# A decoder trunk on one core: chunk 1's attention scores on two PSUM tiles instead of six

## The chip, the cores and the metric

The kernel runs on 1 core of one Trainium2 chip. The metric is the device time of one execution in microseconds (us); less is better. The engines that matter here are TensorE (PE, matmuls), VectorE (DVE), ScalarE (ACT) and GpSimd (POOL); SyncE (SP) issues most DMAs. Matmuls write into PSUM, which the kernel divides into eight tiles of 128 x 512 fp32.

## What is computed

A trunk of two layers on 256 tokens of width 1024. The first layer is a gated MLP over chunks, the second sparse attention with 16 heads in 4 groups. Both are followed by a squared-ReLU MLP of width 4096. Only the attention matters here. With 256 tokens the selected blocks and the window cover all earlier tokens, so that both branches are causal attention over their own keys; a third, small branch goes over compressed keys. Cut from the reference:

```python
def masked_softmax(s, mask):
    s = jnp.where(mask, s.astype(jnp.float32), -jnp.inf)
    m = jnp.max(s, axis=-1, keepdims=True)
    ...
    e = jnp.exp(s - m)
    den = jnp.sum(e, axis=-1, keepdims=True)
    return e / jnp.where(den > 0, den, 1.0)

def nsa_mixer(h, w_in, w_out, k_cmp, v_cmp, k_sel, v_sel, k_win, v_win):
    proj = h @ w_in
    q = proj[..., :HD].reshape(B, T, N_KV_HEADS, HEADS_PER_GROUP, HEAD_DIM) * (HEAD_DIM ** -0.5)
    ...
    s_sel = jnp.einsum('bqghd,bgqmd->bghqm', qb, ks)
    p_sel = masked_softmax(s_sel, kpos <= tq[None, None, None, :, None])
    o_sel = jnp.einsum('bghqm,bgqmd->bqghd', p_sel.astype(vs.dtype), vs)
    ...
    o = gb[..., 0:1] * ocb + gb[..., 1:2] * o_sel + gb[..., 2:3] * o_win
    ...
    return o @ w_out
```

## The kernel before

The 256 tokens are two chunks of 128 (ck = 0 and 1), each on the 128 partitions. Two generators, one for each chunk, run through the same stages, and `drive` (L973) takes turns between them: chunk 0 leads, chunk 1 follows some steps behind and uses the same weights. A scheduler then puts the instructions of each engine in order by priorities and by when it expects data and tiles to be there. So which PSUM tile an instruction waits for sets its place, too. Projections are made of three matmuls a product (`mm3`, L376 to L379: high part of the weight, low part of the weight, low part of the activations).

The eight PSUM tiles are three pools: `psY` with four (output sums, `oT` and `y`), `psA` with two (projections, `pa`; gates; compressed scores, `cs`) and `psT` with two (transposes). A tile of a pool is given out again when all that read its last owner are done.

The attention of a chunk (`nsa`, L921) has two halves p2, with two groups g each. A half goes through:

- `queries` (L780): a projection of 24 matmuls (`pa_bin` in psA), two copies of it (`qs`, high part on ACT at L786, low part on DVE at L787), transposes (`ptq`, L792) and their copies (`qT`).
- `scores` (L822), for each group: chunk 1 makes one score tile for each of four heads (h0 = 0 to 3), chunk 0 one for two heads (h0 = 0 and 2). A tile takes two matmuls against the keys of both branches (L838) and one for the causal mask (L840) per head. DVE takes the negative maxima (`mx`, L841), then ACT the exponentials with their sums (`p` and `den`, L845), one for each head and branch.
- `weighted` (L851): DVE scales p (L866), PE transposes it (`ptp`, L874), ACT copies that (`pT`, L876), and PE sums it with the values into `oT` (L879). The two groups of a half lie side by side as two column tiles of 64, so that their matmuls can run together.
- `attend_cmp` (L884): scores over compressed keys (`cs`, L891, in psA), their softmax on DVE, a transpose (`ptcm`), and a last addition to `oT` (L918).

Afterwards `oT` is split into two parts (`hh_o` on ACT, `hl_o` on DVE) and projected (`nsa_out`, L953, `y_mix`), and the feed-forward stage of the second layer follows.

The table `SY` says which score tiles (ck, g, h0) come from psY; all others come from psA (L833):

```python
sc = (psY.tile([P, per, 2, nk], F32, tag="y", name=f"sc_{ck}_{g}_{h0}") if (ck, g, h0) in SY else
      psA.tile([P, per, 2, nk], F32, tag="a", name=f"sc_{ck}_{g}_{h0}"))
```

The third field of an entry is the head; it is no count of tiles. Before, four tiles of chunk 0 and six of chunk 1 come from psY.

Of the kernel before, what the change touches and what calls it, by code (L numbers as in the profile page):

```python
# [41 lines left out]
PRIA = 100  # L42
PRIS = 150
RAW = 8
SY = [(0, 0, 2), (0, 1, 2), (0, 2, 0), (0, 3, 2), (1, 0, 2), (1, 0, 3), (1, 1, 2), (1, 1, 3), (1, 2, 1), (1, 3, 2)]
PRI = 30
FB = (13, 0.9)
RATES = (1.5, 0.69, 0.9, 0.13)
# [3 lines left out]
def trunk(ctx: ExitStack, tc: tile.TileContext, x, vec, rowv, first_w, ada_w, ada_b, norm_g, a_w_in, a_w_s, a_w_out,  # L52
# [364 lines left out]
    @contextmanager  # L417
    def prio(n):
        if n:
            with tc.high_priority(offset=n):  # L420
                yield
        else:
            yield
# [398 lines left out]
    def scores(ck, g, pool):  # L822
# [8 lines left out]
        for h0 in range(0, 4, per):  # L831
            with prio(PRIS):
                sc = (psY.tile([P, per, 2, nk], F32, tag="y", name=f"sc_{ck}_{g}_{h0}") if (ck, g, h0) in SY else  # L833
                      psA.tile([P, per, 2, nk], F32, tag="a", name=f"sc_{ck}_{g}_{h0}"))
# [283 lines left out]
```

## Time and profile before

| | us |
|---|---|
| median of three runs | 707.84 |
| lowest and highest | 706.71 and 709.61 |
| the profiled execution | 708.93 |
| its span, first to last instruction | 707.2 |

| engine | busy us | share |
|---|---|---|
| PE | 664.2 | 94% |
| DVE | 472.6 | 67% |
| ACT | 354.5 | 50% |
| POOL | 35.6 | 5% |

All times below are counted from the start of the span. The attention runs from about 386 us, when the first scores start, to about 495 us. Chunk 1's scores start at 417.6 us and end at 478 us. A row of the timeline gives the start, the duration, the engine, the line, the instruction with what it writes and reads, and in brackets how long the engine was idle before it and what released it; the profile leaves numbers out of the tiles' names. Matmuls are pipelined: the next one starts before the one ahead of it has ended, so that the distance of starts is what a matmul costs. "Granted clock" is TensorE's clock as a share of 2.4 GHz.

### The profile page before, as it was taken

How to read it: one execution, taken by the hardware profiler on the slowest of the kernel's cores; microseconds unless marked ns; L12 is line 12 of the kernel's file. 1: busy time of each engine (PE TensorE's matmuls, PEld its weight loads, DVE VectorE, ACT ScalarE, POOL GpSimd, SP SyncE). 2: the span in 40 equal slices, each digit the busy share in tenths (PEclk: the TensorE clock that was granted, in tenths of full speed). 3: DMA queues.
4: the chain of work that ended last, by engine and by line, in shares of the span. 5: the costliest groups of instructions: out<-in, count | busy, mean ns of one | idle time of the engine just before them, and what ended most of it. 6: DMA issues, size and time to landing. Idle time of an engine off the chain costs nothing.

```text
span 707.2 us, 9154 instructions
## 1 busy us (share of the span) xinstructions
PE 664.2 (94%) x3296; PEld 501.0 (71%) x3296; DVE 472.6 (67%) x712; ACT 354.5 (50%) x599; POOL 35.6 (5%) x70
## 2 busy tenths in 40 slices
PE   3999988999999999997899989979999999999996
PEld 1556856778888888876658556656778888888884
DVE  3557975997597786868975176754797545455524
ACT  4434435655534543463545386755556555455521
POOL 3002000100000000002000000000120000000000
PEclk9999999999999999998899999999999999999999
DMA  8978978779588988955675882200576656665101
GB/s 336 409 279 341 338 282 310 240 254 371 184 322 303 381 282 319 334 193 179 198 263 186 347 307 90 100 21 1 170 263 225 221 193 209 213 209 201 61 0 61
DMA packets 45535, 162.61 MB, mean 230 GB/s; under 512 B 5417, under 2 KB 5801, under 8 KB 45490
## 3 DMA queue, kind: packets, MB, share of 16 engines
q1 hardware_dynamic: 44928, 161.82, 63.0%
q8 instruction: 26, 0.43, 0.2%
q10 hardware_dynamic: 466, 0.20, 0.1%
q14 instruction: 19, 0.16, 0.1%
q0 software_dynamic: 96, 0.01, 0.0%
HBM read 160.96 MB, written 1.05 MB: 229 GB/s over the span
## 4 chain that ended last, share of the span: by engine, by line
PE 83%; ACT 6%; DMA 4%; DVE 3%; issue 2%; POOL 1%; SPq 0%; ACTq 0%; POOLq 0%; DVEq 0%
PE pa_fi L377 8%; PE pa_fi L379 8%; PE pa_fi L378 8%; PE y_ff L379 8%; PE y_ff L377 8%; PE y_ff L378 8%; PE pa_ain L377 2%; PE pa_ain L378 2%; PE pts_ff L490 2%; PE pa_ain L379 2%; DMA aw_sc<-in_ada_w_dram 2%; PE oT L879 2%; PE sc L838 2%; PE pa_kv L377 1%; PE pa_kv L378 1%
## 5 line engine op out<-in xcount | busy, mean ns | idle before, releaser
L353 DVE TENSOR_TENSOR wl_fo<-w_fo,wh_fo 128x1024 fp32r<-128x1024 f32 x64 | 77.9, 1223 | 54.2 <-ACT wh_fo L352 52.1
L378 PE MATMUL y_ff<-wl_fo,rh_ff 128*128 128x512 f32 x256 | 102.9, 402 | 0.0
L377 PE MATMUL pa_fi<-wh_fi,hh_ff 128*128 128x512 f32 x256 | 100.3, 392 | 1.9 <-ACT hh_ff L382 1.9
L377 PE MATMUL y_ff<-wh_fo,rh_ff 128*128 128x512 f32 x256 | 101.8, 398 | 0.0
L379 PE MATMUL y_ff<-wh_fo,rl_ff 128*128 128x512 f32 x256 | 101.3, 396 | 0.0
L352 ACT ACTIVATE wh_fo<-w_fo 128x1024 fp32r<-128x1024 f32 x64 | 67.3, 1057 | 67.6 <-PE pa_fi L379 50.9
L378 PE MATMUL pa_fi<-wl_fi,hh_ff 128*128 128x512 f32 x256 | 99.9, 390 | 0.0
L379 PE MATMUL pa_fi<-wh_fi,hl_ff 128*128 128x512 f32 x256 | 99.7, 391 | 0.0
L353 DVE TENSOR_TENSOR wl_fi<-w_fi,wh_fi 128x1024 fp32r<-128x1024 f32 x64 | 77.6, 1222 | 31.8 <-ACT wh_fi L352 31.3
L352 ACT ACTIVATE wh_fi<-w_fi 128x1024 fp32r<-128x1024 f32 x64 | 67.1, 1057 | 56.5 <-PE y_ff L379 49.5
L377 PEld LDWEIGHTS pa_fi<-wh_fi,hh_ff 128*128 128x128 f32 x256 | 48.1, 188 | 12.6 <-ACT hh_ff L382 2.8
L377 PEld LDWEIGHTS y_ff<-wh_fo,rh_ff 128*128 128x128 f32 x256 | 48.2, 188 | 10.8
L379 PEld LDWEIGHTS y_ff<-wh_fo,rl_ff 128*128 128x128 f32 x256 | 48.3, 189 | 10.2
L378 PEld LDWEIGHTS y_ff<-wl_fo,rh_ff 128*128 128x128 f32 x256 | 48.4, 189 | 10.0
L379 PEld LDWEIGHTS pa_fi<-wh_fi,hl_ff 128*128 128x128 f32 x256 | 48.1, 188 | 10.1
L378 PEld LDWEIGHTS pa_fi<-wl_fi,hh_ff 128*128 128x128 f32 x256 | 48.1, 188 | 9.9
L504 ACT ACTIVATE r_ff<-pa_fi 128x512 f32<-128x512 f32 x32 | 19.0, 594 | 35.7 <-PE pa_fi L379 35.7
L196 DVE SCALAR_TENSOR_TENSOR acc_g<-aw_g,cact,acc_g 128x1024 f32<-128x1024 f32 x24 | 30.7, 1281 | 5.0 <-DMA aw_g<-in_ada_w_dram 4.0
L845 ACT ACTIVATE p<-sc,mx 128x128 f32<-128x128 f32 (+1 forms) x64 | 26.0, 429 | 8.1 <-DVE mx L841 7.6
L377 PE MATMUL pa_ain<-wh_ain,hh_mix 128*128 128x512 f32 x64 | 26.4, 418 | 2.7 <-ACT hh_mix L382 2.7
L383 DVE TENSOR_TENSOR rl_ff<-pts_ff,rh_ff 128x512 fp32r<-128x512 f32 x32 | 21.9, 686 | 7.7 <-ACT rh_ff L382 7.5
L378 PE MATMUL pa_ain<-wl_ain,hh_mix 128*128 128x512 f32 x64 | 26.3, 414 | 0.0
(291 smaller groups left out, 1157.2 us busy)
## 6 DMA issues: line engine op xcount, KB each, us to landing
w_fi<-in_ff_w_in_dram SPq DMA_DIRECT2D x64, 512.0 KB, 4.7
w_fo<-in_ff_w_out_dram SPq DMA_DIRECT2D x64, 512.0 KB, 4.3
aw_g<-in_ada_w_dram SPq DMA_DIRECT2D x32, 512.0 KB, 4.5
aw_sh<-in_ada_w_dram SPq DMA_DIRECT2D x24, 512.0 KB, 5.3
aw_sc<-in_ada_w_dram SPq DMA_DIRECT2D x24, 512.0 KB, 6.0
aw_first<-in_first_w_dram SPq DMA_DIRECT2D x16, 512.0 KB, 7.7
w_ain<-in_a_w_in_dram SPq DMA_DIRECT2D x16, 512.0 KB, 7.2
w_kv<-in_kv_w_dram SPq DMA_DIRECT2D x12, 512.0 KB, 4.5
```

The costliest lines, as they stand in the source:

```text
L196: nc.vector.scalar_tensor_tensor(acc, raw, cs, acc, ALU.mult, ALU.add)
L352: i1 = nc.scalar.activation(hi[:, :n], raw[:, :n], AF.Copy)
L353: i2 = nc.vector.tensor_tensor(lo[:, :n], raw[:, :n], hi[:, :n].bitcast(F32), ALU.subtract)
L377: nc.tensor.matmul(ps, hh, wh, start=start, stop=False)
L378: nc.tensor.matmul(ps, hh, wl, start=False, stop=False)
L379: nc.tensor.matmul(ps, hl, wh, start=False, stop=stop)
L383: nc.vector.tensor_tensor(lo, src, hi.bitcast(F32), ALU.subtract))
L490: nc.tensor.transpose(pt[:, j * P:(j + 1) * P], src[:, j * P:(j + 1) * P], ident)
L504: nc.scalar.activation(r, pa, AF.Relu)
L838: nc.tensor.matmul(sc[:, i, :, :], qT[:, h0 + i, :], kT[:, g, hl, :, 0:nk], start=(hl == 0), stop=False)
L845: nc.scalar.activation(pr[h0 + i][:, br, :], sc[:, i, br, :], AF.Exp, bias=mx[:, 2 * i + br:2 * i + br + 1], accum_out=den[:, n:n + 1])
L879: m = nc.tensor.matmul(oT[64 * gg:64 * gg + 64, :], V[:, kc, br, g * 64:g * 64 + 64], pTs[gg][0], start=(br == 0 and kc == 0), stop=False)
```

## The change

Six entries of the table go, those of chunk 1. Its sixteen score tiles then all come from psA, which they share with the query projections of both chunks and the compressed scores. Chunk 0's entries stay.

```diff
-SY = [(0, 0, 2), (0, 1, 2), (0, 2, 0), (0, 3, 2), (1, 0, 2), (1, 0, 3), (1, 1, 2), (1, 1, 3), (1, 2, 1), (1, 3, 2)]
+SY = [(0, 0, 2), (0, 1, 2), (0, 2, 0), (0, 3, 2)]
```

No instruction of the computation is added or removed, and the orders of POOL and of SP stay as they were. PE, DVE and ACT get another order between 417 and 500 us. Three places follow. In the names, the first number is the chunk; sc_1_0_2 is chunk 1's score tile of group 0 and head 2, and the last number tells tiles apart.

PE at the start of chunk 1's scores, before: behind cs comes chunk 0's second query projection, pa_bin_512_0 (six matmuls, of which the first three are shown; then come the transposes ptp).

```order
L840 MATMUL sc_1_0_0_3634<-maskn_118,identr_100 128x2x128
L840 MATMUL sc_1_0_1_3657<-maskn_118,identr_100 128x2x128
L838 MATMUL sc_1_0_2_3671<-kT_2863,qT_1_0_0_3614 128x512
L840 MATMUL sc_1_0_2_3671<-maskn_118,identr_100 128x2x128
L891 MATMUL cs_0_0_3733<-kc2_2866,qT_0_0_0_3319 128x32 x4
L891 MATMUL cs_0_0_3733<-kc2_2866,qT_0_0_1_3326 128x32 x4
L377 MATMUL pa_bin_512_0_3781<-wh_bin_512_0_3784,hh_b_0_3153 128x512
L378 MATMUL pa_bin_512_0_3781<-wl_bin_512_0_3785,hh_b_0_3153 128x512
L379 MATMUL pa_bin_512_0_3781<-wh_bin_512_0_3784,hl_b_0_3154 128x512
```

The same place after the change:

```order
L840 MATMUL sc_1_0_0_3634<-maskn_118,identr_100 128x2x128
L838 MATMUL sc_1_0_1_3657<-kT_2863,qT_1_0_0_3614 128x512
L840 MATMUL sc_1_0_1_3657<-maskn_118,identr_100 128x2x128
L838 MATMUL sc_1_0_2_3671<-kT_2863,qT_1_0_0_3614 128x512 x2
L840 MATMUL sc_1_0_2_3671<-maskn_118,identr_100 128x2x128
L891 MATMUL cs_0_0_3733<-kc2_2866,qT_0_0_0_3319 128x32 x4
L891 MATMUL cs_0_0_3733<-kc2_2866,qT_0_0_1_3326 128x32 x4
L874 MATMUL ptp_0_0_0_0_3693<-identr_100,p_0_0_0_3334 128x128
L874 MATMUL ptp_0_0_0_0_3693<-identr_100,p_0_0_1_3335 128x128
```

The matmuls of sc_1_0_2 now come in one piece behind both others, and behind cs come the transposes of p. Six of these transposes and a further score tile, sc_1_0_3, stand ahead of the projection's first matmul.

PE at the end of chunk 0's second projection, before: chunk 1's projection pa_bin_512_1 follows at once, and the query transposes ptq stand behind nine of its matmuls.

```order
L379 MATMUL pa_bin_512_0_3781<-wh_bin_512_3_3863,hl_b_0_3154 128x512
L377 MATMUL pa_bin_512_1_4052<-wh_bin_512_0_3784,hh_b_1_3492 128x512
L378 MATMUL pa_bin_512_1_4052<-wl_bin_512_0_3785,hh_b_1_3492 128x512
L379 MATMUL pa_bin_512_1_4052<-wh_bin_512_0_3784,hl_b_1_3493 128x512
L377 MATMUL pa_bin_512_1_4052<-wh_bin_512_0_3784,hh_b_1_3492 128x512
L378 MATMUL pa_bin_512_1_4052<-wl_bin_512_0_3785,hh_b_1_3492 128x512
L379 MATMUL pa_bin_512_1_4052<-wh_bin_512_0_3784,hl_b_1_3493 128x512
L377 MATMUL pa_bin_512_1_4052<-wh_bin_512_1_3815,hh_b_1_3492 128x512
L378 MATMUL pa_bin_512_1_4052<-wl_bin_512_1_3816,hh_b_1_3492 128x512
L379 MATMUL pa_bin_512_1_4052<-wh_bin_512_1_3815,hl_b_1_3493 128x512
L792 MATMUL ptq_0_1_0_3885<-identr_100,qs_0_1_3881 128x128 x4
L792 MATMUL ptq_0_1_1_3892<-identr_100,qs_0_1_3881 128x128 x4
```

The same place after the change:

```order
L377 MATMUL pa_bin_512_0_3781<-wh_bin_512_3_3863,hh_b_0_3153 128x512
L378 MATMUL pa_bin_512_0_3781<-wl_bin_512_3_3864,hh_b_0_3153 128x512
L379 MATMUL pa_bin_512_0_3781<-wh_bin_512_3_3863,hl_b_0_3154 128x512
L838 MATMUL sc_1_1_3_3873<-kT_2863,qT_1_0_1_3621 128x512 x2
L840 MATMUL sc_1_1_3_3873<-maskn_118,identr_100 128x2x128
L891 MATMUL cs_1_0_4014<-kc2_2866,qT_1_0_0_3614 128x32 x4
L891 MATMUL cs_1_0_4014<-kc2_2866,qT_1_0_1_3621 128x32 x4
L792 MATMUL ptq_0_1_0_3885<-identr_100,qs_0_1_3881 128x128 x4
L792 MATMUL ptq_0_1_1_3892<-identr_100,qs_0_1_3881 128x128 x4
L377 MATMUL pa_bin_512_1_4052<-wh_bin_512_0_3784,hh_b_1_3492 128x512
```

Between the last matmul of pa_bin_512_0 and ptq now stand the last score tile of group 1 and cs_1_0; chunk 1's projection comes behind ptq. On DVE, at the same place, before:

```order
L841 TENSOR_REDUCE mx_1_1_2_3854<-sc_1_1_2_3853 128x2
L841 TENSOR_REDUCE mx_1_1_3_3874<-sc_1_1_3_3873 128x2
L895 TENSOR_TENSOR sm_1_0_4023<-cs_1_0_4014,cneg_126 128x128
L896 TENSOR_TENSOR sm_1_0_4023<-cs_1_0_4014,sm_1_0_4023 128x128
L383 TENSOR_TENSOR hl_o_0_4261<-oT_0_0_3333,hh_o_0_4260 128x512
L787 SCALAR_TENSOR_TENSOR qs_0_1_3881<-pa_bin_512_0_3781,qs_0_1_3881 128x8x64
```

and after the change:

```order
L841 TENSOR_REDUCE mx_1_1_2_3854<-sc_1_1_2_3853 128x2
L383 TENSOR_TENSOR hl_o_0_4261<-oT_0_0_3333,hh_o_0_4260 128x512
L841 TENSOR_REDUCE mx_1_1_3_3874<-sc_1_1_3_3873 128x2
L787 SCALAR_TENSOR_TENSOR qs_0_1_3881<-pa_bin_512_0_3781,qs_0_1_3881 128x8x64
L895 TENSOR_TENSOR sm_1_0_4023<-cs_1_0_4014,cneg_126 128x128
L896 TENSOR_TENSOR sm_1_0_4023<-cs_1_0_4014,sm_1_0_4023 128x128
```

The split of oT (hl_o) and the maxima of sc_1_1_3 now stand directly ahead of the copy qs_0_1, and cs's softmax (sm) behind it.

PE at the end of chunk 1's first half, before: the last sums oT of group pair 0 and, at once, the query transposes.

```order
L874 MATMUL ptp_1_1_1_1_4005<-identr_100,p_1_1_3_3803 128x128
L879 MATMUL oT_1_0_3628<-pT_1_0_1_1_4003,V_2864 64x512
L879 MATMUL oT_1_0_3628<-pT_1_1_1_1_4010,V_2864 64x512
L918 MATMUL oT_1_0_3628<-pcT_1_0_4042,vc_3486 64x128 x8
L792 MATMUL ptq_1_1_0_4112<-identr_100,qs_1_1_4108 128x128 x4
L792 MATMUL ptq_1_1_1_4119<-identr_100,qs_1_1_4108 128x128 x4
```

The same place after the change:

```order
L874 MATMUL ptp_1_1_1_1_4005<-identr_100,p_1_1_3_3803 128x128
L379 MATMUL pa_bin_512_1_4052<-wh_bin_512_3_3863,hl_b_1_3493 128x512
L912 MATMUL ptcm_1_0_4039<-identr_100,pc_1_0_4036 128x128 x2
L377 MATMUL pa_bin_512_1_4052<-wh_bin_512_3_3863,hh_b_1_3492 128x512
L879 MATMUL oT_1_0_3628<-pT_1_0_1_1_4003,V_2864 64x512
L879 MATMUL oT_1_0_3628<-pT_1_1_1_1_4010,V_2864 64x512
L918 MATMUL oT_1_0_3628<-pcT_1_0_4042,vc_3486 64x128 x8
L378 MATMUL pa_bin_512_1_4052<-wl_bin_512_3_3864,hh_b_1_3492 128x512
L379 MATMUL pa_bin_512_1_4052<-wh_bin_512_3_3863,hl_b_1_3493 128x512
L792 MATMUL ptq_1_1_0_4112<-identr_100,qs_1_1_4108 128x128 x4
L792 MATMUL ptq_1_1_1_4119<-identr_100,qs_1_1_4108 128x128 x4
```

The last four matmuls of chunk 1's projection now stand around the last sums oT, two of them directly ahead of ptq_1_1, which transposes this projection.

## Rows read from the trace of the kernel before

**Rows 1.** The page: engines (busy, share, instructions) and the chain by engine.

```profile
PE 664.2 (94%) x3296; PEld 501.0 (71%) x3296; DVE 472.6 (67%) x712; ACT 354.5 (50%) x599; POOL 35.6 (5%) x70
...
PE 83%; ACT 6%; DMA 4%; DVE 3%; issue 2%; POOL 1%; SPq 0%; ACTq 0%; POOLq 0%; DVEq 0%
```

**Rows 2.** Stretches: length, busy us by engine, granted clock, DMA share, GB/s.

```profile
416.00:436.00 20.00, 16.61 (x78) 11.87 (x79) 15.01 (x42) 14.92 (x42) 0.31 (x1) 0.91 0.57 208
436.00:444.00 8.00, 7.99 (x57) 6.12 (x55) 4.10 (x8) 5.37 (x16) 0.00 (x0) 1.00 0.10 37
444.00:462.00 18.00, 16.40 (x113) 11.13 (x111) 12.89 (x39) 13.04 (x41) 0.31 (x1) 1.00 0.34 118
462.00:475.00 13.00, 9.25 (x48) 6.59 (x47) 9.36 (x36) 8.23 (x31) 0.00 (x0) 0.87 0.00 0
...
540.00:707.20 167.20, 160.95 (x726) 130.05 (x723) 83.16 (x81) 74.50 (x98) 1.72 (x4) 0.99 0.46 158
```

**Rows 3.** The same view around the two falls of the granted clock.

```profile
420.80:424.20 3.40, 1.93 (x12) 1.70 (x13) 3.40 (x8) 3.40 (x14) 0.00 (x0) 1.00 0.81 329
424.20:427.60 3.40, 3.40 (x12) 2.62 (x11) 3.19 (x18) 2.29 (x9) 0.00 (x0) 0.51 0.50 159
465.20:468.60 3.40, 1.14 (x9) 1.07 (x9) 3.09 (x10) 3.02 (x15) 0.00 (x0) 1.00 0.00 0
468.60:472.00 3.40, 3.38 (x11) 2.44 (x11) 2.72 (x15) 1.57 (x8) 0.00 (x0) 0.50 0.00 0
```

**Rows 4.** PE in time: start, us, what, [idle before it and releaser].

```profile
416.41 0.87 PE L792 MATMUL ptq<-identr,qs 128*128 128x128 f32 x8 [0.48 <-DVE qs L787]
...
421.07 1.07 PE L891 MATMUL cs<-kc,qT 128*128 128x32 f32 x8 [1.43 <-ACT p L845]
...
423.34 0.50 PE L377 MATMUL pa_bin<-wh_bin,hh_b 128*128 128x512 f32 x1 [1.20 <-ACT p L845]
```

**Rows 5.** DVE and ACT behind the first score tile (start, us, what).

```profile
419.21 0.69 DVE L841 TENSOR_REDUCE mx<-sc 128x2 f32<-128x512 f32 x1 [1.38 <-PE sc L840]
...
419.99 0.47 ACT L845 ACTIVATE p<-sc,mx 128x256 f32<-128x256 f32 x1
...
420.81 0.20 ACT L845 ACTIVATION_READ_ACCUMULATOR p<-sc,mx 128x1 f32 x1
```

**Rows 6.** PE in time, the pair oT_0_0 of chunk 0.

```profile
429.87 1.07 PE L879 MATMUL oT<-pT,V 128*64 128x512 f32 x2
...
431.65 1.07 PE L879 MATMUL oT<-pT,V 128*64 128x512 f32 x2
```

**Rows 7.** PE in time, chunk 1, from 450 to 470 us.

```profile
450.56 1.08 PE L879 MATMUL oT<-pT,V 128*64 128x512 f32 x4 [0.26 <-ACT pT L876]
...
457.16 1.08 PE L879 MATMUL oT<-pT,V 128*64 128x512 f32 x4 [0.60 <-ACT pT L876]
...
459.79 1.08 PE L879 MATMUL oT<-pT,V 128*64 128x512 f32 x4 [0.75 <-ACT pT L876]
...
466.66 1.06 PE L891 MATMUL cs<-kc,qT 128*128 128x32 f32 x8 [1.72 <-ACT p L845]
...
468.52 1.11 PE L838 MATMUL sc<-kT,qT 128*128 128x512 f32 x2 [0.80 <-DVE sm L896]
...
469.93 0.77 PE L838 MATMUL sc<-kT,qT 128*128 128x512 f32 x1
```

**Rows 8.** ACT and DVE: copies of the queries, two maxima in a row.

```profile
415.03 0.60 ACT L786 ACTIVATE qs<-pa_bin 128x512 fp32r<-128x512 f32 x1 [1.18 <-PE pa_bin L379]
...
415.66 0.69 DVE L787 SCALAR_TENSOR_TENSOR qs<-pa_bin,qs 128x512 fp32r<-128x512 f32 x1 [0.37 <-ACT qs L786]
...
464.86 1.29 DVE L841 TENSOR_REDUCE mx<-sc 128x2 f32<-128x512 f32 x2 [1.75 <-PE sc L840]
```

**Rows 9.** PE in time, dense projection matmuls.

```profile
441.00 0.39 PE L377 MATMUL pa_bin<-wh_bin,hh_b 128*128 128x512 f32 x1
441.23 0.39 PE L378 MATMUL pa_bin<-wl_bin,hh_b 128*128 128x512 f32 x1
```

## The prediction

> **What bounds the kernel now.** I read the page first, for the share of the engines and the chain that ended last. TensorE (PE) is busy for 664.2 of 707.2 us, and 83% of the chain lies on it [rows 1]. So an edit counts by how much PE work it adds and by how long PE waits. The change touches only the attention of the second layer, so the next view is the table of stretches [rows 2]. The reader is to see where PE is not full. In 436 to 444 us it is busy 7.99 of 8.00 us. In the three other stretches of attention it is not: 16.61 of 20.00, 16.40 of 18.00 and 9.25 of 13.00 us, which leaves 3.4, 1.6 and 3.75 us idle. After 540 us it is busy 160.95 of 167.20 us: there is hardly a hole there in which a delay could be made up. The third view is the granted clock in short stretches [rows 3]. It is at 1.00 (2.4 GHz) except in 424.20 to 427.60 and 468.60 to 472.00, where it is 0.51 and 0.50 (1.2 GHz). Ahead of these two, PE was busy 1.93 and 1.14 of 3.40 us. The fourth view is PE's own timeline, which names each wait [rows 4, 6 and 7].
>
> **What the wait for a PSUM tile costs.** A score tile is free again when VectorE (DVE) has taken its maxima and ScalarE (ACT) has read it twice. In the rows: 0.69 us for the maxima from 419.21, then two exponentials from 419.99 to 421.01 [rows 5], 1.8 us in all. The query projection's tile is free after two copies, 0.60 us on ACT and 0.69 us on DVE, from 415.03 to 416.35 [rows 8]. The next transposes then started at 416.41 [rows 4].
>
> **The change part by part.** No instruction is added or removed and no DMA moves: SP's queue and POOL's keep their order. What changes is which PSUM tile six score tiles of chunk 1 wait for, and with it the order in which the scheduler puts PE, DVE and ACT. A dense projection matmul costs 0.23 us from start to start [rows 9].
>
> 1. Third head of chunk 1's first group (sc_1_0_2). Before, it had a tile of its own, and PE waited 1.43 us ahead of cs_0_0 and 1.20 us ahead of the projection [rows 4]. The six projection matmuls then ran while DVE scaled the first p tiles. Now sc_1_0_2 itself waits for the exponentials that cs_0_0 waited for, cs_0_0 for the next two, and behind cs_0_0 the transposes of p come at once, since the projection has no tile yet. The two old waits stay. What is new is that 6 x 0.23 = 1.38 us of work no longer stands in front of the transposes, which DVE paces. At best DVE is ready earlier and half is kept (+0.7). At worst all is lost and the following transposes also go at DVE's pace (+1.8). I take +1.4, nearer to the upper end, because DVE is busy 3.40 of 3.40 us there [rows 3].
>
> 2. The pair of output matmuls. Before, oT_0_0's two column tiles were torn apart by the three matmuls of sc_1_0_3: 1.07 us alone at 429.87, and 1.07 us alone at 431.65 [rows 6]. Where the two stand side by side, both together take 1.08 us [rows 7]. Now this pair stands side by side: -1.0 us.
>
> 3. End of chunk 0's second projection. Before, nine projection matmuls of chunk 1 covered the copies of qs, and PE had no hole between 436 and 444 us [rows 2]. Now those nine cannot start, because pa_bin_512_1 needs a tile that sc_1_1_3 holds. PE does the three matmuls of sc_1_1_3 and then stands at cs_1_0, which waits for DVE's copy qs_0_1. DVE does the maxima of sc_1_1_3 first: 1.29 us for two such steps in a row [rows 8], with qs of 0.69 us as the second, plus the hand-overs. That is +1.4 at least, and +2.0 if hl_o, which now stands ahead of both on DVE, delays them. I take +1.7. Behind cs_1_0 on PE stand the query transposes, then chunk 1's projection: all wait with it.
>
> 4. The holes of chunk 1's first half. PE waited 0.26, 0.60 and 0.75 us for ACT's copies of pT [rows 7], 1.61 us together. The projection matmuls that come later now stand there, four of them right in front of the last two of these waits (4 x 0.23 = 0.9). I take -1.5 (bounds -0.9 and -1.6), since the earlier ones shift the whole stretch as well.
>
> 5. End of chunk 1's projection. Its last two matmuls now stand directly ahead of the transposes ptq_1_1, which need both copies of qs. Before, the projection was over ahead of the three waits of item 4, and this cost nothing. The price is the row of the only place where the copies are seen with a wait: 415.03 to 416.41, 1.4 us [rows 4, 8]. It is +1.4 if DVE is free and +2.0 if hl_o stands ahead of it there too. I take +1.7; everything of chunk 1's second half is queued behind it on PE.
>
> 6. Chunk 1's second half. The third tile sc_1_2_2 now waits for the exponentials, where cs_0_1 waited 1.72 us, and cs_0_1 then waits about as long as sc_1_2_3 did (0.80 us) [rows 7]. One wait for another: +0.1 (bounds -0.3 and +0.5). The later tiles of g = 3 have output-projection matmuls between them, so I cost them at nothing. If that cover were too short, a wait would be at most the 1.8 us of one tile, less the matmuls between.
>
> Sum: 1.4 - 1.0 + 1.7 - 1.5 + 1.7 + 0.1 = +2.4 us. By the lower ends it is 0.7 - 1.0 + 1.4 - 1.6 + 1.4 - 0.3 = +0.6, by the upper ends 1.8 - 1.0 + 2.0 - 0.9 + 2.0 + 0.5 = +4.4.
>
> 7. The clock. Both falls follow a stretch in which PE mostly waited [rows 3]. Items 3 and 5 put two new waits of that kind into a part in which the clock is now at 1.00. I take one further stretch of 3.4 us at the lower level. If it were full of matmuls it would lose half, 1.7 us: a score matmul took 0.77 us at the lower clock against 0.39 us for an equally wide matmul at the upper [rows 7, 9]. Since the waits lie in it, where the clock costs nothing, I take half of that, +0.8 (bounds 0 and 1.7 for each such stretch).
>
> The Trainium skill, "TensorE: Matmul & The Clock Gate", section "A second HAM failure mode: psum-queue depth-cycling", tells of a kernel that cycles through PSUM banks, in which PE idles briefly between groups of matmuls so often that the clock goes up and down. That rule speaks against this change, and by it the fourth case below would be the result; the trace agrees in so far as both falls lie beside waits for PSUM tiles [rows 3, 4, 7]. The same page, section "HAM oscillation — how this bites in real kernels", reports that PSUM double-buffering gave no further gain in its kernel. By that the sum would be nothing, the second case; the rows neither show nor exclude it, since PE waits for tiles before the change too.
>
> With the clock the change costs 2.4 + 0.8 = +3.2 us. The profiled execution took 708.93 us (span 707.2), so it would be 712.1. The median of the three runs is 707.84, 1.1 us below it, and there it gives **711.0 us**.
>
> **The rivals.**
> - *As worked out*, 711.0 (709.5 to 712.6): each end of the sum moves it by about 1.8 us, but not all ends fall together. Chance 0.58.
> - *The waits only change places*, 707.8 (706.8 to 709): the new waits at items 3 and 5 cover what DVE and ACT would have been waited for a little later, and the clock does not fall again. For it speaks that DVE is busy 9.36 of 13.00 us in 462 to 475 [rows 2], so that PE would have to wait for it anyway. Against it speaks that 436 to 444 us has no hole now. Chance 0.18.
> - *The moved projections cover everything*, 705.4: items 2 and 4 give their 2.5 us and items 3 and 5 cost nothing. That needs the copies of qs to end within the three matmuls that stand between, 0.7 us against 1.4 us in the rows, or DVE to be free at once. Chance 0.05.
> - *The clock falls twice more, and the stretches are full*, 713.6: 2.4 + 2 x 1.7 = +5.8. It decides from the point at which the stretch behind item 3 falls as well as one behind item 5. For it speaks that PE already waits 1.72 and 0.80 us right behind item 5 [rows 7]. Chance 0.19.
>
> **How the numbers follow.** A measurement of this kernel can tell about 0.5% from no change, 3.5 us, so slower begins at 711.4. Of the first case some four tenths lie above that (0.23), with the last case 0.42. Faster is the third case alone, 0.05. The rest, 0.53, is within. The range 707.3 to 713.4 leaves out the third case, a little of the second's lower end, and about half of the last.
>
> **What would show it.** In the profile of the changed kernel PE should wait 1.4 to 2 us for DVE's qs at cs (L891, chunk 1, near 440 us) and again at ptq (L792, near 463 us). sc (L838) should wait for ACT's p near 421 and 467 us. No oT pair should be torn apart near 430 us, and the waits of oT for pT between 450 and 460 us should be gone. The attention's last oT should end 2 to 4 us later than now, and all that follows should be shifted by the same. It is wrong if ptq finds its qs ready, if the feed-forward stage makes up the delay, or if the granted clock shows fewer falls than now.

## The result and the profile after

The changed kernel takes 715.0 us (median of seven runs, 711.88 to 717.95) against 707.84 us before (seven runs, 705.7 to 709.61). The ratio is 1.0103, with a 95% interval of 1.0079 to 1.0126: it is about 7.2 us slower. The forecast was 711.0 us, and the result lies 1.6 us above the upper end of its range.

The profiled execution took 717.95 us, its span is 716.2 us. The page's engines and the chain by engine, as in [rows 1], hardly moved:

```profile
PE 670.5 (94%) x3296; PEld 505.5 (71%) x3296; DVE 474.1 (66%) x712; ACT 355.4 (50%) x599; POOL 35.8 (5%) x70
...
PE 83%; ACT 5%; DVE 4%; DMA 3%; issue 2%; POOL 1%; SPq 0%; ACTq 0%; DVEq 0%; POOLq 0%
```

PE has the same 3296 matmuls and is busy 6.3 us longer. Work that is the same and takes longer points to the clock. This execution is the slowest of the seven, so that what it shows of the clock is more than a usual run has; the experiments come back to this. First the waits, in PE's timeline of the changed kernel (start, us, what, [idle before it and releaser]). This execution was 1.7 us behind that of before when the attention began: ptq of chunk 1 stands at 418.11, in [rows 4] at 416.41.

```profile
418.11 0.87 PE L792 MATMUL ptq<-identr,qs 128*128 128x128 f32 x8 [0.48 <-DVE qs L787]
...
422.62 0.73 PE L838 MATMUL sc<-kT,qT 128*128 128x512 f32 x2 [1.87 <-ACT p L845]
...
424.67 1.89 PE L891 MATMUL cs<-kc,qT 128*128 128x32 f32 x8 [1.20 <-ACT p L845]
427.22 1.54 PE L874 MATMUL ptp<-identr,p 128*128 128x128 f32 x6 [0.66 <-DVE p L866]
...
431.31 1.08 PE L879 MATMUL oT<-pT,V 128*64 128x512 f32 x4
...
445.03 1.04 PE L891 MATMUL cs<-kc,qT 128*128 128x32 f32 x8 [1.87 <-DVE qs L787]
...
469.08 0.89 PE L792 MATMUL ptq<-identr,qs 128*128 128x128 f32 x8 [1.78 <-DVE qs L787]
...
473.87 1.22 PE L838 MATMUL sc<-kT,qT 128*128 128x512 f32 x2 [1.84 <-ACT p L845]
...
475.48 1.89 PE L891 MATMUL cs<-kc,qT 128*128 128x32 f32 x8 [0.18 <-ACT p L845]
```

Each wait stands where the prediction put it: sc_1_0_2 (1.87 us), cs_1_0 (1.87), ptq_1_1 (1.78), sc_1_2_2 (1.84). The pair oT_0_0 is together at 431.31 (four matmuls in 1.08 us, in [rows 6] two of them took 1.07). The three waits of oT in [rows 7] are gone. The stretches of [rows 2], of the changed kernel (length, busy us by engine, granted clock, DMA share, GB/s):

```profile
416.00:436.00 20.00, 15.45 (x78) 10.53 (x77) 16.40 (x43) 15.42 (x42) 0.31 (x1) 0.83 0.59 209
436.00:444.00 8.00, 7.16 (x43) 5.07 (x39) 2.51 (x5) 3.54 (x12) 0.00 (x0) 1.00 0.19 67
444.00:462.00 18.00, 16.93 (x101) 13.10 (x102) 13.01 (x41) 12.80 (x40) 0.46 (x1) 0.91 0.14 46
462.00:475.00 13.00, 8.87 (x53) 5.39 (x52) 4.40 (x6) 6.79 (x19) 0.00 (x0) 0.86 0.29 100
475.00:495.00 20.00, 19.13 (x107) 14.70 (x107) 14.94 (x62) 11.94 (x41) 0.31 (x1) 0.84 0.00 1
```

The column behind POOL is the granted clock: 0.83, 0.91 and 0.84 in three of five stretches. Before it was 0.91 and 1.00 in the first two of these three [rows 2], and 1.00 in the last:

```profile
475.00:495.00 20.00, 19.84 (x132) 13.21 (x132) 9.39 (x36) 10.61 (x32) 0.31 (x1) 1.00 0.01 2
```

In finer steps, the changed kernel again, as in [rows 3]:

```profile
420.20:423.60 3.40, 1.40 (x7) 0.71 (x5) 3.16 (x5) 3.07 (x11) 0.00 (x0) 0.99 0.97 377
423.60:427.00 3.40, 1.89 (x8) 1.78 (x8) 2.34 (x8) 3.40 (x15) 0.00 (x0) 0.50 0.90 331
427.00:430.40 3.40, 3.18 (x13) 2.75 (x13) 3.40 (x18) 1.45 (x5) 0.00 (x0) 0.51 0.09 31
...
444.00:447.40 3.40, 2.37 (x20) 2.15 (x21) 1.47 (x4) 1.94 (x6) 0.00 (x0) 1.00 0.00 0
447.40:450.80 3.40, 3.40 (x17) 3.40 (x17) 2.18 (x10) 1.62 (x9) 0.00 (x0) 0.50 0.00 0
...
468.00:471.40 3.40, 1.97 (x13) 1.61 (x13) 2.25 (x3) 2.22 (x4) 0.00 (x0) 0.99 0.03 6
471.40:474.80 3.40, 1.56 (x5) 1.17 (x4) 1.89 (x3) 2.00 (x10) 0.00 (x0) 0.50 0.41 151
474.80:478.20 3.40, 3.22 (x14) 2.72 (x13) 2.63 (x11) 2.35 (x12) 0.00 (x0) 0.50 0.00 0
478.20:481.60 3.40, 3.40 (x14) 3.01 (x14) 3.28 (x18) 0.80 (x2) 0.00 (x0) 0.51 0.02 5
```

TensorE is at 1.2 GHz (0.50) in six such stretches, 20.4 us, against two, 6.8 us, before. Ahead of each of the three falls PE had waited for a tile of psA or for qs: it was busy 1.40, 2.37 and 1.97 of 3.40 us there. PE is busy for 16.65 us of those six stretches, which at 2.4 GHz would take up to 8.3 us less; before it was 6.78 us [rows 3], up to 3.4 us. So the clock could account for up to 4.9 us of the loss, and the forecast had 0.8 for it.

Where the loss arises is seen by one measure that is free of what ran ahead of the attention: from the first score of chunk 1 to the last output-projection matmul. In each kernel everything that the change puts in another order lies between them. The last start is read from the view of the tile y_mix (shortest, median and longest duration in ns, then the first and the last start), here of the changed kernel:

```profile
L379 PE MATMUL y_mix<-wh_bout,hl_o x32: 387/389/486, 484.3 to 522.1; 128*128 128x512 f32 x32
```

and of the kernel before:

```profile
L379 PE MATMUL y_mix<-wh_bout,hl_o x32: 387/389/481, 477.2 to 513.0; 128*128 128x512 f32 x32
```

That is 522.1 - 419.3 = 102.8 us against 513.0 - 417.6 = 95.4 us, **7.4 us more**. From there to the end of the span it is 194.1 to 194.3 us in every kernel of this study: nothing is made up later, and nothing more is lost.

### The profile page after: what moved, and what is told of

It reads as the page before. It is cut to its first block, busy times and chain, and to the rows that moved or that the text cites. A ratio compares the mean times of both kernels' runs of the same rounds, so it can differ in the third digit from the quotient of the medians.

```text
span 716.2 us, 9167 instructions
## 1 busy us (share of the span) xinstructions
PE 670.5 (94%) x3296; PEld 505.5 (71%) x3296; DVE 474.1 (66%) x712; ACT 355.4 (50%) x599; POOL 35.8 (5%) x70
## 4 chain that ended last, share of the span: by engine, by line
PE 83%; ACT 5%; DVE 4%; DMA 3%; issue 2%; POOL 1%; SPq 0%; ACTq 0%; DVEq 0%; POOLq 0%
PE pa_fi L377 8%; PE pa_fi L379 8%; PE pa_fi L378 8%; PE y_ff L379 8%; PE y_ff L377 8%; PE y_ff L378 8%; PE pa_ain L377 2%; PE pa_ain L378 2%; PE pa_ain L379 2%; PE pts_ff L490 2%; DMA aw_sc<-in_ada_w_dram 2%; PE sc L838 2%; PE ptp L874 2%; PE oT L879 2%; PE pa_kv L377 1%
## 5 line engine op out<-in xcount | busy, mean ns | idle before, releaser
L379 PEld LDWEIGHTS y_ff<-wh_fo,rl_ff 128*128 128x128 f32 x256 | 48.3, 189 | 10.2
```

The costliest lines, as they stand in the source:

```text
L379: nc.tensor.matmul(ps, hl, wh, start=False, stop=stop)
```

## The experiments

Theory A: the waits cost some 2.4 us, and the rest is the clock, which falls because PE stands still more often. Theory B: the waits and the new order cost all of it, and the clock is a companion.

To tell them apart, some kernels put **dummy matmuls** into the waits. They multiply the keys by the identity (0.23 us each from start to start) and write into a PSUM tile of the transposes, ahead of the transposes that own it and overwrite it. A table says ahead of which tile and how many; where they then run on PE is up to the scheduler and is seen in the rows:

```diff
+    def dummy(pt, n):
+        for _ in range(n): nc.tensor.matmul(pt.bitcast(F32), identr, at["kT"][:, 0, 0, :, :], start=True, stop=True)
...
-            pt = pt_tile(f"ptq_{ck}_{b}_{gg}", F32R)
+            pt = pt_tile(f"ptq_{ck}_{b}_{gg}", F32R); dummy(pt, FILL.get(f"ptq_{ck}_{b}_{gg}", 0))
...
-                    pt = pt_tile(f"ptp_{ck}_{g}_{br}_{kc}")
+                    pt = pt_tile(f"ptp_{ck}_{g}_{br}_{kc}"); dummy(pt, FILL.get(f"ptp_{ck}_{g}_{br}_{kc}", 0))
```

Their rows have the line L83. The results together; the ratios are to runs of the kernel before on the same chip. "Attention" is the length defined above and "1.2 GHz" the time at the lower level in it, both of the one profiled execution. The last column is the time at the lower level in the whole span, as a mean of all runs, and the same of the kernel before on that chip. It is worked out from each run's mean granted clock c, as 2 x (1 - c) x span. For the profiled executions of before, the change, e1 and e9 this gives 24.0, 37.2, 17.0 and 7.0 us, where the stretches of their profiles add up to 23.6, 36.7, 16.8 and 7.0.

| kernel | median us, before | ratio (95%) | attention us | 1.2 GHz us | all runs, before |
|---|---|---|---|---|---|
| before | 707.84 | | 95.4 | 6.8 | |
| the change | 715.0, 707.84 | 1.0103 (1.0079 to 1.0126) | 102.8 | 20.4 | 32.0 |
| e1, change, four waits filled | 709.32, 706.74 | 1.0039 (1.0021 to 1.0058) | 99.0 | 6.8 | 16.2, 20.0 |
| e2, four entries of the first half out | 714.59, 706.74 | 1.0125 (1.0097 to 1.0153) | 102.6 | 20.4 | 31.9, 20.0 |
| e3, two entries of the second half out | 707.77, 706.74 | 1.0008 (0.9990 to 1.0026) | 95.4 | 6.8 | 21.5, 20.0 |
| e4, before, one wait filled | 704.22, 706.74 | 0.9968 (0.9951 to 0.9985) | 95.1 | 6.8 | 12.8, 20.0 |
| e5, change, waits of sc filled | 712.13, 707.75 | 1.0079 (1.0051 to 1.0106) | 100.6 | 10.2 | 19.4, 20.3 |
| e6, change, waits for qs filled | 712.71, 707.75 | 1.0084 (1.0056 to 1.0112) | 100.6 | 13.6 | 23.9, 20.3 |
| e7, two entries of group 1 out | 714.36, 707.75 | 1.0106 (1.0072 to 1.0140) | 101.8 | 13.6 | 30.4, 20.3 |
| e8, two entries of group 0 out | 708.27, 707.75 | 1.0015 (0.9992 to 1.0038) | 96.7 | 10.2 | 23.2, 20.3 |
| e9, e7 with its wait filled | 710.61, 707.26 | 1.0051 (1.0032 to 1.0069) | 96.4 | 0 | 18.9, 20.4 |
| e10, before, two waits filled | 706.0, 707.26 | 0.9988 (0.9966 to 1.0010) | 94.2 | 3.4 | 16.7, 20.4 |
| e11, before, three waits filled | 705.11, 707.26 | 0.9965 (0.9947 to 0.9982) | 93.5 | 0 | 12.2, 20.4 |

**e1: the four waits filled.**

```diff
+FILL = {'ptp_0_0_0_0': 8, 'ptq_0_1_0': 8, 'ptq_1_1_0': 7, 'ptp_0_2_0_0': 8}
```

> The changed kernel, and in four of its waits 31 matmuls (8, 8, 7 and 8) that write into a PSUM tile of the transposes just ahead of its real owner, which overwrites them; nothing of the computation is left out. They stand ahead of sc_1_0_2 (wait 1.87 us), cs_1_0 (1.87), ptq_1_1 (1.78) and sc_1_2_2 (1.84); DVE, ACT and the queues keep their order. 31 x 0.23 us = 7.1 us of work into 7.4 us of waits. Theory A (the waits alone are 2.4 us, and the other 5 of the 7.2 us come from the clock, which falls because PE stands still): the lower level shrinks from 20 us in the attention to 0 to 7, and the time to 709 to 711 us. Theory B (the waits and the new order cost all of it; the clock is only a companion): 714.5 to 716, or longer by as much as the dummies overrun their waits.

709.32 us, a ratio of 1.0039 against 1.0103: with 7.1 us of additional PE work the changed kernel is 0.64%, 4.5 us, faster. The dummies fit the waits. PE in time of e1, at sc_1_0_2 and at cs_1_0:

```profile
415.14 2.02 PE L83 MATMUL ptp<-kT,identr 128*128 128x512 f32 x8
417.16 0.73 PE L838 MATMUL sc<-kT,qT 128*128 128x512 f32 x2
...
436.80 2.03 PE L83 MATMUL ptq<-kT,identr 128*128 128x512 f32 x8
438.83 1.04 PE L891 MATMUL cs<-kc,qT 128*128 128x32 f32 x8
```

From the last matmul of sc_1_0_1 to the first of sc_1_0_2 it is 2.13 us in e1 and 2.15 us in the change: the tile comes free when it did, and nothing was shortened but PE's idleness. What did change is the clock. The short stretches of e1:

```profile
417.20:420.60 3.40, 1.88 (x11) 1.41 (x11) 3.17 (x9) 3.15 (x13) 0.00 (x0) 1.00 0.81 296
420.60:424.00 3.40, 3.05 (x12) 2.61 (x13) 3.40 (x19) 2.40 (x8) 0.00 (x0) 0.53 0.32 125
...
437.40:440.80 3.40, 3.40 (x25) 2.71 (x23) 1.87 (x5) 1.53 (x6) 0.00 (x0) 1.00 0.00 0
440.80:444.20 3.40, 3.40 (x26) 2.83 (x24) 2.24 (x11) 2.08 (x10) 0.00 (x0) 1.00 0.00 0
...
465.20:468.60 3.40, 2.64 (x17) 1.82 (x16) 2.53 (x9) 3.34 (x17) 0.00 (x0) 1.00 0.08 25
468.60:472.00 3.40, 3.40 (x14) 3.01 (x14) 3.39 (x19) 1.42 (x6) 0.00 (x0) 0.50 0.00 0
```

The fall behind cs_1_0 is gone (1.00 from 437.40 to 444.20), and of the others one stretch each is left, behind waits that were not filled (1.21 and 0.66 us near 419, 0.76 us near 467). All runs say the same: 16.2 us at the lower level on the mean against 32.0. Theory B falls.

**e5 and e6: the same dummies, two waits at a time.**

```diff
+FILL = {'ptp_0_0_0_0': 8, 'ptp_0_2_0_0': 8}   # e5
+FILL = {'ptq_0_1_0': 8, 'ptq_1_1_0': 7}       # e6
```

> The changed kernel with dummy matmuls in two of the four waits alone: 8 ahead of sc_1_0_2 and 8 ahead of sc_1_2_2, not ahead of cs_1_0 and ptq_1_1; nothing of the computation is left out. The theory that the clock falls wherever PE stands: the falls near 447 us and behind ptq_1_1 (items 3 and 5) stay, those near 423 us and 474 us get shorter, 711 to 713 us against 715.0 of the change and 709.3 with all four filled. The rival, that items 3 and 5 alone let the clock fall: no gain, 714 to 715.

> The other two waits alone: 8 dummies ahead of cs_1_0 (item 3) and 7 ahead of ptq_1_1 (item 5), none at the score tiles; nothing of the computation is left out. The theory that the clock falls wherever PE stands: the fall near 447 us goes, the two at the score tiles stay (6.8 us near 423, and one behind 471): 711 to 713 us. The rival, that items 3 and 5 alone let the clock fall: about the 709.3 us of all four.

712.13 and 712.71 us: each median lies between the change and e1, as expected of a clock that falls wherever PE stands. The intervals of both overlap with that of the change, so that one pair filled is not clearly a gain. Against e1 each pair that is left unfilled costs 0.4% (1.0079 and 1.0084 against 1.0039), which is about as much as the intervals can tell. In e5 the lower level still comes from 444 us, behind the unfilled wait at cs_1_0; in e6 it does not, but lasts 6.8 us from 420.5 and 6.8 us from 468.3 us. The stretch at 444 us in e5, then that of e6:

```profile
444.10:447.50 3.40, 3.40 (x17) 3.40 (x17) 2.22 (x10) 1.67 (x9) 0.00 (x0) 0.51 0.00 0
...
443.50:446.90 3.40, 3.40 (x24) 2.82 (x24) 1.97 (x10) 2.09 (x9) 0.00 (x0) 1.00 0.00 0
```

So the waits of items 3 and 5 alone were not the cause. One thing does not fit: the runs of e5 have no more time at the lower level than those of before (19.4 and 20.3 us), and yet are 0.79% slower. Its stretch at 444 us is full of matmuls, which makes it dear, but that this accounts for all of it isn't shown.

**e2 and e3: one half of the attention at a time.**

```diff
-SY = [..., (1, 0, 2), (1, 0, 3), (1, 1, 2), (1, 1, 3), (1, 2, 1), (1, 3, 2)]
+SY = [..., (1, 2, 1), (1, 3, 2)]   # e2
+SY = [..., (1, 0, 2), (1, 0, 3), (1, 1, 2), (1, 1, 3)]   # e3
```

> Only the four entries of chunk 1's first half are taken out (1,0,2), (1,0,3), (1,1,2), (1,1,3); the two of the second half stay. Items 1 to 5 of the prediction sum to +2.3 us, item 6 is gone. Theory A: +2.3 for the waits and two to three further stretches at the lower clock at 1.6 us each (423 and 447 us, perhaps one behind ptq_1_1): 713 to 715 us. Theory B without the clock: 710 to 711 us. If the second half carries the loss, 708 us.

> Only the two entries of chunk 1's second half are taken out (1,2,1), (1,3,2); the four of the first half stay. Item 6 alone: +0.1 us, 708 us, with the fall of the clock near 469 us as before the change. Theory A: behind the wait of sc_1_2_2 one or two further stretches at the lower clock, 709 to 711 us. If the second half carries the loss, 712 us or more.

714.59 and 707.77 us. The first half carries the whole loss, and the second none that can be told from zero, as item 6 said. The 10.2 us at 1.2 GHz from 471 us in the changed kernel don't need the second half's new order: e2 has them too, behind the wait of ptq_1_1 (1.78 us), though its second half is ordered as before:

```profile
467.50:477.70 10.20, 7.51 (x26) 5.90 (x24) 6.15 (x24) 4.84 (x22) 0.00 (x0) 0.50 0.16 51
```

**e7 and e8: one group of the first half at a time.**

```diff
-SY = [..., (1, 0, 2), (1, 0, 3), (1, 1, 2), (1, 1, 3), (1, 2, 1), (1, 3, 2)]
+SY = [..., (1, 0, 2), (1, 0, 3), (1, 2, 1), (1, 3, 2)]   # e7
+SY = [..., (1, 1, 2), (1, 1, 3), (1, 2, 1), (1, 3, 2)]   # e8
```

> Only the entries (1,1,2) and (1,1,3) are taken out. In the order of PE this has item 3 (cs_1_0 and ptq wait for the copies qs_0_1) and most of item 4, but not item 5: the projection of chunk 1 ends ahead of the last oT. By the waits alone +1.7 - 0.9 = +0.8, 707.5 us; with one further stretch at the lower clock near 447 us +1.6 more, 709 us. If item 5 is what costs, 707 us.

> Only the entries (1,0,2) and (1,0,3) are taken out. This has items 1 and 2 (sc_1_0_2 waits, and the pair oT_0_0 stands together), and none of items 3 to 5. By the waits alone +1.4 - 1.0 = +0.4, 707.1 us; with one further stretch of 3.4 us at the lower clock near 424 us, 708.7 us.

e8 came out as expected, 708.27 us, no loss that can be told from zero: the third head's wait and the mended pair nearly cancel. e7 did not: 714.36 us against 707.5 to 709. Its PE in time shows two reasons:

```profile
433.53 1.07 PE L879 MATMUL oT<-pT,V 128*64 128x512 f32 x2
...
434.90 1.07 PE L879 MATMUL oT<-pT,V 128*64 128x512 f32 x2
...
442.87 0.70 PE L838 MATMUL sc<-kT,qT 128*128 128x512 f32 x2 [1.89 <-DVE qs L787]
```

Here the scheduler (the "planner" of the expectations) tears a second pair of oT apart, as it did the first in [rows 6]: each half takes 1.07 us, where four matmuls side by side take 1.08. And behind the wait of 1.89 us the clock lies low through two stretches in which PE is never idle:

```profile
444.00:447.40 3.40, 3.40 (x17) 3.11 (x17) 1.00 (x3) 2.08 (x6) 0.00 (x0) 0.50 0.00 0
447.40:450.80 3.40, 3.40 (x18) 3.30 (x17) 1.75 (x9) 1.03 (x6) 0.00 (x0) 0.50 0.00 0
```

Two full stretches lose half of 6.8 us, 3.4. With 1.9 for the wait and 1.0 for the pair, less the 0.60 us of a wait of oT that is filled here, that is 5.7 of the 6.4 us by which its attention is longer. In the other places it has two stretches at the lower level, as before.

**e9: that wait filled.**

```diff
+SY = [..., (1, 0, 2), (1, 0, 3), (1, 2, 1), (1, 3, 2)]
+FILL = {'ptq_0_1_0': 8}
```

> The entries (1,1,2) and (1,1,3) alone taken out, as in e7 (714.4 us), and 8 dummy matmuls in the wait of 1.89 us that this order has behind sc_1_1_2; nothing of the computation is left out. If this one wait is what lets the clock fall for the 6.8 us from 444 us (6.7 us of PE work in them), the fall goes and the time drops by 2 to 3.4 us to 711 to 712 us. What stays is then the wait itself and the second torn pair of oT_0_0, 3 to 4 us over the kernel before. If the fall does not hang on this wait: 714.

710.61 us, a ratio of 1.0051 against 1.0106: one filled wait, of the same length as in e7, gives back half of the loss, somewhat more than the 2 to 3.4 us expected. The short stretches of e9 there, and at the next waits:

```profile
437.40:440.80 3.40, 3.29 (x24) 2.63 (x23) 1.73 (x4) 2.13 (x9) 0.00 (x0) 1.00 0.00 0
440.80:444.20 3.40, 3.40 (x25) 2.95 (x24) 1.87 (x9) 1.92 (x9) 0.00 (x0) 1.00 0.00 0
...
464.20:467.60 3.40, 1.73 (x12) 1.57 (x13) 3.10 (x12) 3.40 (x17) 0.00 (x0) 1.00 0.00 0
467.60:471.00 3.40, 2.46 (x19) 1.80 (x19) 3.40 (x18) 2.15 (x8) 0.00 (x0) 1.00 0.02 5
```

The fall is gone. But this execution, 706.16 us, is the fastest of e9's twelve, with nothing at the lower level in its attention. On the mean of all runs e9 has 18.9 us at that level and e7 30.4, so e9 is back at the 20.4 of the kernel before, and the 0.51% by which it is still slower are, by this measure, waits and order. In this execution the waits of 1.72 and 0.80 us in the second half, which are those of [rows 7], let no fall follow either (1.00 from 464.20 to 471.00), while in the profile of before they did [rows 3].

**e4, e10 and e11: the kernel before, its own waits filled.**

```diff
+FILL = {'ptp_0_2_0_0': 7}   # e4
+FILL = {'ptp_0_2_0_0': 7, 'ptp_0_3_0_0': 3}   # e10
+FILL = {'ptp_0_0_0_0': 5, 'ptp_0_2_0_0': 7, 'ptp_0_3_0_0': 3}   # e11
```

> The kernel before, with 7 dummy matmuls (1.6 us) in the wait of 1.72 us ahead of cs_0_1 at 464.9 us; nothing of the computation is left out. Theory A: the 3.4 us at the lower clock from 468.6 us go, and with them 1.7 us of the 3.4 us of work in them: 706 to 707 us. Theory B: 708 us, no change.

> The kernel before with dummies in both waits of chunk 1's second half: 7 and 1 ahead of cs_0_1 (1.72 us), 2 behind it (wait of 0.80 us); nothing of the computation is left out. With 7 alone it was 704.2 against 706.7 us. The clock theory: the same or a few tenths less, 703.5 to 704.5 us. If the 8th delays cs_0_1: 0.2 more.

> As e10, with 5 more dummies in the wait of 1.43 us ahead of cs_0_0; nothing of the computation is left out. The planner then changes the order of 21 VectorE instructions, too. The clock theory: the fall near 424 us goes or is put off, up to 1.7 us less than e10: 702 to 703.5 us. If the new order of VectorE costs as much, the same as e10 or more.

e4 and e11 are faster than the kernel before by about 0.3%, 704.22 and 705.11 us, with dummies that compute nothing. The 2.5 us of e4 are more than the 1.7 us that its expectation gave the fall behind the filled wait. e11's gain, 2.5 us by its ratio, falls short of its forecast of 702 to 703.5 us, and its order on VectorE is another one, so that it is no pure test. e10 missed its forecast of 703.5 to 704.5 with 706.0 us; its interval reaches from 0.9966 to 1.0010, so that it neither agrees nor clearly disagrees with e4.

The profile of e4 shows why one execution is not enough. The fall behind the filled wait is gone, but the fall at the start of chunk 1's scores lasts 6.8 us in place of the 3.4 us of [rows 3]:

```profile
420.30:423.70 3.40, 2.25 (x6) 1.75 (x7) 3.40 (x13) 3.40 (x17) 0.00 (x0) 0.50 0.55 208
423.70:427.10 3.40, 3.40 (x12) 2.65 (x12) 2.38 (x15) 1.07 (x3) 0.00 (x0) 0.51 0.44 153
...
467.70:471.10 3.40, 2.97 (x18) 2.18 (x18) 3.40 (x19) 2.05 (x10) 0.00 (x0) 1.00 0.02 5
```

This is the second slowest of e4's twelve runs, and its attention (95.1 us) shows next to nothing of the gain. On the mean of all runs e4 has 12.8 us at the lower level against 20.0.

## Why the prediction was wrong

**How the 7.4 us divide.** Order the kernels with the changed first half by their time at 1.2 GHz: e1 has 6.8 us there and an attention of 99.0 us, the change 20.4 and 102.8: 3.8 us for 13.6 us at the lower level, 0.28 us per us. The kernel before gives the same slope: e11 has 0 us and 93.5, before 6.8 and 95.4. e9 and e7 give a steeper one, 5.4 us for 13.6, 0.40. At an equal 6.8 us the change (e1) lies 99.0 - 95.4 = 3.6 us above before. So about **3.6 us are waits and order, and 3.8 us are the clock**. These are single executions.

By all runs the change lies 7.3 us above before, with 32.0 us at the lower level in the whole span, and e1 2.8 us, with 16.2: again 0.28 us per us. The kernel before has 20.0 us (29 runs on the chip of e1), more than e1. At its 20.0 us the changed order would lie 2.8 + 0.28 x 3.8 = 3.9 us above it, which leaves 3.4 for the clock. Both are estimates, good to about 1 us: among the runs of one kernel the time grows by only 0.20 us per us at the lower level, though there the stretches outside the attention count too. The forecast had 2.4 for the waits and 0.8 for the clock. So of the 4.1 or 4.2 us that it lacked, 2.6 to 3.0 are the clock and 1.2 to 1.5 the waits.

**The step that failed is item 7.** The price of a stretch came out near: +0.8 taken, 0.28 x 3.4 = 0.95 measured. That is in part luck, since it was a halving without a row behind it, and e7 and e9 give 0.40 x 3.4 = 1.4. The number of stretches was wrong: one further stretch was taken, there were four in the profiled execution, and by all runs 12.0 us more, three and a half. I allowed one fall for the two new waits for qs, items 3 and 5, and none for the waits of items 1 and 6, because those replaced or joined waits that were there. The runs show falls behind the waits of either pair when the other is filled (e5, e6), and that the clock can stay low for more than one stretch: 6.8 us from 423.6 around waits of 1.87 and 1.20 us, 10.2 us from 471.4 around 1.78 and 1.84 us, and in e7 6.8 us behind a single wait of 1.89 us. There PE has only dense work behind the wait, and a stretch costs its full 1.7 us.

The rival "the clock falls twice more", 713.6 us, had 3.4 us for the clock, from two full stretches where there were four that were not full. It came nearest, and what it lacked are the waits. The third rival's 705.4 us took items 2 and 4 and left out the +1.5 us of items 1 and 6; it was not what happened in any case.

The Trainium skill, "TensorE: Matmul & The Clock Gate", section "A second HAM failure mode: psum-queue depth-cycling", tells of something close to this: PE idles briefly between groups of matmuls while it cycles through PSUM banks, and the clock goes up and down. The traces agree, with waits of 1.2 to 1.9 us and 20.4 against 6.8 us at 1.2 GHz, though two of the four waits are for the copies qs and not for a PSUM tile. The section "HAM oscillation — how this bites in real kernels" of that page reports no further gain from PSUM double-buffering in its kernel; here two tiles in place of six for these scores cost 1.0%.

**Items 1 to 6, +2.4 taken.** By e1 against before, at an equal time at 1.2 GHz, they are +3.6, within the bounds of +0.6 to +4.4. In parts, from the starts of the query transposes ptq in both profiles:
- *Items 1 to 3*, +2.1 taken. From the first score of chunk 1 to ptq_0_1 it is 25.85 us in e1. Before it was 25.42, of which nine projection matmuls (2.07 us) that now come later are taken off: +2.5. The wait of item 3 was 1.87 us (1.7 taken), and the pair of item 2 stands together. That a torn pair costs 1.0 us is seen once more in e7.
- *Items 4 and 5*, +0.2 taken. From ptq_0_1 to ptq_1_1 it is 21.66 us in e1 and 18.62 + 2.07 before: +1.0. The wait of item 5 was 1.78 us (1.7 taken), so item 4 gave back only some 0.8 of 1.5 us. The waits themselves did go as taken: outside the wait of item 5 PE is idle for 0.17 us in e1 between these points and was for 1.61 before. What took part of it back are the distances of starts: the 24 projection matmuls take 6.88 us in e1 against 6.23 before, since most of them now stand singly among other matmuls (0.31 us to the next one in place of 0.23), and the score matmuls 0.57 us more, the transposes 0.76 us less.
- *Item 6*, +0.1 taken. From ptq_1_1 to the last y_mix 51.52 us in e1 against 51.33: +0.2, and no loss in e3.

Why the waits for qs are as long as 1.8 us is seen on DVE of the changed kernel at cs_1_0:

```profile
443.00 0.69 DVE L383 TENSOR_TENSOR hl_o<-oT,hh_o 128x512 fp32r<-128x512 f32 x1 [1.79 <-ACT hh_o L382]
443.60 0.68 DVE L841 TENSOR_REDUCE mx<-sc 128x2 f32<-128x512 f32 x1
444.20 0.68 DVE L787 SCALAR_TENSOR_TENSOR qs<-pa_bin,qs 128x512 fp32r<-128x512 f32 x1
```

Behind the last projection matmul hl_o and the maxima run first and the copy third, as item 3 had it at its upper end.

**The signs named in the prediction.** The waits at L891 and L792, those of sc for p, the whole pair and the vanished waits of oT all came. The last oT was to end 2 to 4 us later; against the start of the scores it is 8.1 us later (493.60 and 503.37). The attention is only 7.4 us longer, so the output projection makes up 0.7 us; behind it nothing is made up, as said.

## What to carry to other kernels

A wait of PE of one to two microseconds in a dense stretch costs its own length and, with some chance, a stretch of the following work at half the clock; here the second cost about as much as the first. So count, beside the sum of the waits, how many places there are at which PE stands, and what dense work lies behind each. Matmuls whose result is overwritten, put into the waits without changing the order, tell the two costs apart, and can be worth leaving in (0.3% of the kernel before).

## What the runs showed that was not expected

- More PE work made a kernel faster: 31 matmuls, 7.1 us, took 4.5 us off the changed kernel (e1), and 7 matmuls 2.5 us off the kernel before (e4).
- The same waits in the same order let the clock fall in one execution and not in another. The waits of 1.43 and about 1.2 us at the start of chunk 1's scores [rows 4] are the same in before, e4, e7, e9 and e10, and so is PE's order around them. Behind them the lower level lasted 3.4, 6.8, 3.4, 0 and 3.4 us. So a profile shows that a wait can let the clock fall, and only many runs show how much it costs.
- Two entries of the table (e7) cost as much as all six (1.0106 and 1.0103), since the scheduler answers with another order each time, here with a second torn pair of output sums.
